# A two-block layer on one core: the last product by seven half products, a wide convolution, ScalarE's own gate function

## The chip, the cores and the metric

The kernel runs on one core of one Trainium2 chip. The core has engines that run side by side and wait for each other by semaphores: TensorE (PE) multiplies, VectorE (DVE) and ScalarE (ACT) do element-wise work, GpSimd (POOL) and SyncE (SP) here mostly issue DMAs; ACT issues DMAs too. Each engine takes its instructions strictly in the order in which they were built. The metric is the device time of one execution in microseconds, the median of several runs.

## What is computed

One input x of 1024 positions by 1024 channels goes through a hybrid layer (block 1: four branches, gates, an MLP) and then through block 2, which the change touches. Cut to what matters:

```python
def mix(h, lp, h0, pool_fn):
    proj = einsum('btd,de->bte', h, lp['w_in'])               # 1024 -> 11 slots of 512
    (va, za, bb, bc, bv, zb, ca, cg, zc, dv, zd) = split(proj, 11)
    ya, h_final = rglru(va, lp, h0)                            # mixer a
    yb = bb * depthwise_conv(bc * bv, lp['b_conv'])            # mixer b, 3 taps
    u = depthwise_conv(ca * sigmoid(cg), lp['c_conv'])         # mixer c, 31 taps
    u = layer_norm(u, ...)
    yc = einsum('btc,ce->bte', silu(u), lp['c_pw']) + lp['c_pw_b']
    yd = grouped_linear(pool_grid(dv)) * lp['d_scale']         # mixer d
    cat = concatenate([ya * silu(za), yb * silu(zb), yc * silu(zc), yd * silu(zd)])
    return einsum('bte,ed->btd', cat, lp['w_out'])             # 2048 -> 1024

x = x + gate * mix(h, ...)
return rms_norm(x, final_g)
```

## The kernel before, in words

Activations lie transposed, channels on the 128 partitions and positions along the row, so a tile of one channel group is 128 x 1024, and a half of it (512 positions, one PSUM bank) is called a half tile. Every fp32 product is made of three matmuls in fp32r: both operands are split into a high part (a cast on ACT) and the rest (a subtraction on DVE), and high by high, high by low and low by high are added up in PSUM (lines 411 to 413). One matmul has weights of 128 x 128 and 512 columns.

`mixers_in` (from line 2028) is block 2's input product: 44 weight blocks (11 slots by 4 channel groups), each with two halves of 24 matmuls, `mm<-kk,wh` in the rows. Between the groups `fill` advances generators: `self.bg` holds mixers a and d, and `convs` the 31-tap convolution of mixer c (`conv31`, line 2006 on). That convolution keeps two PSUM banks and adds one tap after the other into them on DVE, 512 columns at a time (line 2025), then copies the result back. Gates are made as 0.5 (1 + tanh(z/2)) z: a Tanh on ACT (lines 1991 and 2092) and a multiplication on DVE (lines 1992 and 2093). Each finished piece of `cat` (256 KB, `cz` or `sg` in the rows) is stored to DRAM by a DMA on ACT's queue.

`tail` (line 2216) is the last product. `dense(pair, hf)` runs four times, for two pairs of mixers and two halves of the positions: eight loads of `cat` (`cr<-cat`, SP's queue), their splits (`cx`, lines 469 and 470), then for each of eight output groups 24 matmuls and one DVE instruction that adds the result times the gate to x (line 2239). x itself was put into DRAM (`x2d`) and is loaded in the first two `dense` calls. `final` is the closing norm of one half.

Three small rings of tiles matter: half tiles (`F2`, six of them, shared by `pk`, `sg`, `cz` and `cr`), weights (three raw, three split) and PSUM (two `mm`, one `px`, five `pp` banks). A DMA into a tile of a ring waits until the tile's former content has been read, by a store too. `weight_sums` (line 1507) makes sums of weight blocks for the Strassen scheme that block 1's MLP uses already: on POOL's queue, load a block, add others by accumulating DMAs, store each partial sum to DRAM, all in one buffer `ws`.

The instructions of an engine do not stand in the order of the source: the framework reorders them when it builds the program, by its own estimates, so the order of the built program is shown below where it matters.

Of the kernel before, what the change touches and what calls it, by code (L numbers as in the profile page):

```python
# [17 lines left out]
P = 128  # L18
T = 1024
# [9 lines left out]
NL, N1, N2, N4, N3, FA, FB = 6.0, 3.0, 3.0, 2.4, 2.5, 4.0, 3.0  # L29
# [272 lines left out]
class Build:  # L302
    def __init__(self, tc, ctx, A, out, dbg=None):
# [16 lines left out]
        self.sums, self.paced = self.weight_sums(), 0  # L320
# [54 lines left out]
    def load_w(self, src, w=T):  # L375
# [3 lines left out]
        self.split(raw[:, :w], hi[:, :w], lo[:, :w])  # L379
        return hi, lo  # L380

    def weight_order(self):
# [9 lines left out]
        q += [("wo2", pair, n) for pair in range(2) for hf in range(2) for n in range(8)]  # L392
        self.wq, self.ahead = q, []

    def take(self, *key):
        if self.wq[0] is None:
            self.wq.pop(0)
        assert self.wq.pop(0) == key
        load = lambda name, *i: self.load_w(self.A[name][i] if name == "wup" else
                                               self.A[name][i].rearrange("p k n -> p (k n)"))  # L400
# [1106 lines left out]
    def weight_sums(self):  # L1507

        nc = self.nc
        A = self.A["wm2"]  # L1510
        self.ws = {n: [self.dp.tile([P, T], F32, name=f"{n}w{j}") for j in range(8)] for n in ("S1", "S2", "S3", "S4")}
        pin = self.tc.keep_in_program_order
        for j in range(8):
            block = lambda a, b: A[a, b][:, j * T:j * T + T]
            for first, *terms in (((1, 0), (1, 1), "S1", (0, 0), "S2", (0, 1), "S4"), ((0, 0), (1, 0), "S3")):
                t = self.wsp.tile([P, T], F32, tag="ws", name=self.nm("ws"))
                pin(nc.gpsimd.dma_start(t, block(*first)))
                yield
                for x in terms:
                    if isinstance(x, str):  # L1520
                        pin(nc.gpsimd.dma_start(self.ws[x][j], t))
                    else:
                        pin(nc.gpsimd.dma_start(t, block(*x), accum_op=ALU.add))
# [459 lines left out]
    def keep(self, slot, c, silu=False):  # L1983
# [15 lines left out]
    def cat_out(self, i, c, y, z, hf):  # L1999
# [3 lines left out]
        self.nc.vector.scalar_tensor_tensor(t, y, 0.5, t, op0=ALU.mult, op1=ALU.mult)  # L2003
        self.cat_store(i, c, t, hf)

# [5 lines left out]
    def conv31(self, c, u):  # L2011

        nc = self.nc
        w = lambda j: self.CW[:, 31 * c + j:31 * c + j + 1]
        acc = [self.pp(), self.pp()]
        for hf, sl in enumerate(HS):
            nc.vector.tensor_scalar(acc[hf], u[:, sl], w(15), None, op0=ALU.mult)
        for j in range(31):
# [3 lines left out]
            for hf in range(2):  # L2022
                a, b = max(HALF * hf, -s), min(HALF * hf + HALF, T - s)
# [292 lines left out]
```

## Time and profile before

| | |
|---|---|
| median of 3 runs | 2543.75 us (2543.48 to 2548.24) |
| profiled execution | 2544.9 us, of which the trace spans 2543.1 |
| PE busy | 2476.3 us, 97% of the span |
| DVE, ACT, POOL busy | 1727.1, 1188.1, 182.1 us (68%, 47%, 7%) |
| DMA traffic | 449 MB, 177 GB/s on average |
| mean granted clock of PE | 0.983 |

The trace of the profiled execution is read in four ways here: the page (totals), windows (busy time of each engine in a stretch, with the number of instructions, the granted clock and the DMA engines' share), timelines (single instructions with their start, their duration and, in brackets, how long the engine had been idle before and what released it), and lists of groups or transfers. Block 2's input product runs from about 1774 to 2329 us and the last product from 2333 to 2527; the closing norm takes the rest.

### The profile page before, as it was taken

The page shows a single profiled execution, that of the slowest core. Times are in us where ns is not written, and L with a number is a line of the kernel's source. Part 1 is how long each engine was busy: PE and PEld are TensorE (multiplying, and loading weights), DVE is VectorE, ACT ScalarE, POOL GpSimd, SP SyncE. Part 2 cuts the span into 40 slices and gives each one's busy share as a digit, 9 for nine tenths or more (in the row PEclk, how much of TensorE's full clock was granted, in tenths as well). Part 3 has the DMA queues.
Part 4 walks back from the last instruction along what each step waited for, and adds up shares of the span by engine and source line. Part 5 has one row for each costly group of instructions (what it writes and reads, how often), then busy time and mean ns, then how long its engine had stood idle before and what let it go on. Part 6 is the DMA issues. An engine that isn't in the chain of part 4 may idle for free. (4 is left out here: it accounts for less than half of the span.)

```text
span 2543.1 us, 33781 instructions
## 1 busy us (share of the span) xinstructions
PE 2476.3 (97%) x12732; PEld 2004.7 (79%) x12732; DVE 1727.1 (68%) x2647; ACT 1188.1 (47%) x1843; POOL 182.1 (7%) x238
## 2 busy tenths in 40 slices
PE   8999999999999999999999999999999999999997
PEld 7887888776777678877788888887888888887886
DVE  7536765664755436758867864457798999996744
ACT  5425554622514357147644543435536355445623
POOL 0000000120111111630000000000000000000000
PEclk9999999999999799999999999999999999999998
DMA  6365443683775567868676565556533333325732
GB/s 218 106 210 160 140 134 105 186 250 104 230 205 157 164 210 233 287 193 278 235 257 221 180 204 180 187 187 224 183 119 113 133 134 97 113 91 192 247 100 100
DMA packets 180085, 449.23 MB, mean 177 GB/s; under 512 B 32145, under 2 KB 42257, under 8 KB 179921
## 3 DMA queue, kind: packets, MB, share of 16 engines
q1 hardware_dynamic: 141504, 342.44, 40.5%
q0 software_dynamic: 18576, 64.63, 9.1%
q10 hardware_dynamic: 19840, 40.00, 4.3%
q8 instruction: 100, 1.64, 0.3%
q14 instruction: 65, 0.52, 0.1%
HBM read 321.55 MB, written 125.44 MB: 176 GB/s over the span
## 5 line engine op out<-in xcount | busy, mean ns | idle before, releaser
L367 ACT CAST wh<-wr 128x1024 fp32r<-128x1024 f32 x243 | 255.0, 1049 | 496.3 <-PE mm L412 246.5
L368 DVE TENSOR_TENSOR wl<-wr,wh 128x1024 fp32r<-128x1024 f32 x243 | 299.5, 1233 | 222.4 <-ACT wh L367 215.9
L411 PE MATMUL mm<-h,wh 128*128 128x512 f32 x760 | 308.1, 406 | 4.0 <-ACT h L469 2.1
L412 PE MATMUL mm<-h,wh 128*128 128x512 f32 x760 | 305.9, 403 | 0.8 <-DVE h L470 0.8
L413 PE MATMUL mm<-h,wl 128*128 128x512 f32 x760 | 304.7, 401 | 0.0
L411 PE MATMUL mm<-kk,wh 128*128 128x512 f32 x704 | 275.2, 391 | 0.0
L412 PE MATMUL mm<-kk,wh 128*128 128x512 f32 x704 | 274.5, 390 | 0.5 <-DVE kk L1811 0.5
L413 PE MATMUL mm<-kk,wl 128*128 128x512 f32 x704 | 274.0, 389 | 0.0
L411 PEld LDWEIGHTS mm<-h,wh 128*128 128x128 f32 x760 | 144.9, 191 | 37.2 <-ACT h L469 3.3
L412 PEld LDWEIGHTS mm<-h,wh 128*128 128x128 f32 x760 | 144.9, 191 | 33.7 <-issue 3.6
L413 PEld LDWEIGHTS mm<-h,wl 128*128 128x128 f32 x760 | 144.6, 190 | 32.7 <-issue 2.9
L2025 DVE SCALAR_TENSOR_TENSOR pp<-cu,vec,pp 128x512 f32<-128x512 f32 (+9 forms) x240 | 166.3, 746 | 0.1
L412 PEld LDWEIGHTS mm<-kk,wh 128*128 128x128 f32 x704 | 132.1, 188 | 29.1 <-issue 1.0
L411 PEld LDWEIGHTS mm<-kk,wh 128*128 128x128 f32 x704 | 132.1, 188 | 28.3 <-issue 0.7
L413 PEld LDWEIGHTS mm<-kk,wl 128*128 128x128 f32 x704 | 132.1, 188 | 27.7 <-issue 0.2
L1539 PE MATMUL pp<-h,wh 128*128 128x512 f32 x320 | 126.2, 397 | 3.8 <-ACT x L1606 2.2
L1540 PE MATMUL pp<-h,wh 128*128 128x512 f32 x320 | 124.8, 390 | 1.4 <-DVE h L470 1.4
L1541 PE MATMUL pp<-h,wl 128*128 128x512 f32 x320 | 123.6, 389 | 0.0
L1748 PE MATMUL pp<-bl,wh 128*128 128x512 f32 x304 | 120.1, 395 | 2.4 <-DVE bl L470 1.7
L1749 PE MATMUL pp<-bh,wl 128*128 128x512 f32 x304 | 119.1, 392 | 0.0
L1747 PE MATMUL pp<-bh,wh 128*128 128x512 f32 x304 | 116.5, 391 | 1.6 <-ACT bh L474 1.6
L411 PE MATMUL mm<-cx,wh 128*128 128x512 f32 x256 | 99.8, 391 | 1.3 <-ACT cx L469 1.3
(562 smaller groups left out, 5434.8 us busy)
## 6 DMA issues: line engine op xcount, KB each, us to landing
wr<-in_wi_dram SPq DMA_DIRECT2D x77, 512.0 KB, 3.4
ws<-in_wm_dram POOLq DMA_DIRECT2D x48, 512.0 KB, 5.8
wr<-in_wo_dram SPq DMA_DIRECT2D x48, 512.0 KB, 3.7
wr<-in_wg_dram SPq DMA_DIRECT2D x32, 512.0 KB, 4.4
gt<-gt POOLq DMA_DIRECT2D x64, 256.0 KB, 4.6
g<-gt SPq DMA_DIRECT2D x64, 256.0 KB, 4.9
wm<-in_wm_dram SPq DMA_DIRECT2D x32, 512.0 KB, 5.0
br<-buB SPq DMA_DIRECT2D x32, 512.0 KB
```

The costliest lines, as they stand in the source:

```text
L367: self.nc.scalar.copy(hi, raw)
L368: self.nc.vector.tensor_sub(lo, raw, hi.bitcast(F32))
L411: M(ps, lhsT=ah, rhs=bh, start=start and i == 0, stop=False)
L412: M(ps, lhsT=ah, rhs=bl, start=False, stop=False)
L413: M(ps, lhsT=al, rhs=bh, start=False, stop=stop and i == last)
L1539: M(ps, lhsT=ah, rhs=bh, start=start and i == 0, stop=False, skip_group_check=True)
L1540: M(ps, lhsT=ah, rhs=bl, start=False, stop=False, skip_group_check=True)
L1541: M(ps, lhsT=al, rhs=bh, start=False, stop=i == last, skip_group_check=True)
L1747: M(banks[p], lhsT=wh[:, o], rhs=bh[:, r], start=first, stop=False, skip_group_check=True)
L1748: M(banks[p], lhsT=wh[:, o], rhs=bl[:, r], start=False, stop=False, skip_group_check=True)
L1749: M(banks[p], lhsT=wl[:, o], rhs=bh[:, r], start=False, stop=jj == 7 and e == 1, skip_group_check=True)
L2025: nc.vector.scalar_tensor_tensor(o, u[:, a + s:b + s], w(j), o, op0=ALU.mult, op1=ALU.add)
```

## The change

1. The last product is done by Strassen's scheme over 2 x 2 blocks: the inputs are cut into two pairs of mixers (1024 channels each), the outputs into two groups of 512 channels, the positions into two halves. Seven products P1, P5, P2, P6, P7, P4, P3 of 4 output tiles x 8 operands x 3 matmuls take the place of eight. P1 stays in four PSUM banks and P2 is added onto it; P5 stays in four others until P3 is added; P6, P7 and P4 are added up in the first four again. Operands that are sums or differences of two pieces of `cat` are made by a load and an accumulating DMA on POOL's queue (`ct` and part of `cr`). The signs of the pieces are set where they are made (`sign_of`).
2. The weights of P5, P6, P7 and P3 are sums of blocks of `w_out`, made by a second `weight_sums` (4 output tiles): 40 more DMAs of 512 KB on POOL's queue.
3. x is loaded behind P1.
4. The convolution works in SBUF on 1023 columns or so at a time instead of 512 in PSUM, with its first tap on ACT; the LayerNorm and pointwise product of mixer c (`mixer_c`) are queued right behind the convolutions, not at the last loop's end.
5. The gates use ACT's Silu; the DVE multiplication of each goes.

```diff
-NL, N1, N2, N4, N3, FA, FB = 6.0, 3.0, 3.0, 2.4, 2.5, 4.0, 3.0
+NL, N1, N2, N4, N3, FA, FB = 6.0, 3.0, 3.0, 2.4, 2.5, 4.0, 4.0
...
             if silu:
-                nc.scalar.activation(t, ps, AF.Tanh, scale=0.5)
-                nc.vector.scalar_tensor_tensor(t, t, 1.0, ps, op0=ALU.add, op1=ALU.mult)
+                nc.scalar.activation(t, ps, AF.Silu)
...
-    def conv31(self, c, u):
+    def conv31(self, c, us):
...
-        acc = [self.pp(), self.pp()]
-        for hf, sl in enumerate(HS):
-            nc.vector.tensor_scalar(acc[hf], u[:, sl], w(15), None, op0=ALU.mult)
+        o = self.S("co")
+        nc.scalar.mul(o, u, w(15))
...
-            for hf in range(2):
-                a, b = max(HALF * hf, -s), min(HALF * hf + HALF, T - s)
-                o = acc[hf][:, a - HALF * hf:b - HALF * hf]
-                nc.vector.scalar_tensor_tensor(o, u[:, a + s:b + s], w(j), o, op0=ALU.mult, op1=ALU.add)
-            yield 1.3
-        for hf, sl in enumerate(HS):
-            nc.scalar.copy(u[:, sl], acc[hf])
+            a, b = max(0, -s), min(T, T - s)
+            nc.vector.scalar_tensor_tensor(o[:, a:b], u[:, a + s:b + s], w(j), o[:, a:b], op0=ALU.mult, op1=ALU.add)
+            yield 1.2
+        us[c] = o
...
+        self.sums = self.weight_sums(4, lambda a, b, j: self.A["wo2"][b, 4 * a + j].rearrange("p k n -> p (k n)"))
...
+            if c == 3:
+                convs.append(self.mixer_c(cus))
...
-            if c == 3:
-                while convs:
-                    self.tick(1, convs)
-                self.behind(self.mixer_c(cus))
...
     def tail(self):
...
-        def dense(pair, hf, ticks):
-            cx = HiLo.__new__(HiLo)
-            cx.t = [[], []]
-            for i in ((0, 3), (1, 2))[pair]:
-                for c in range(4):
-                    raw = self.F2("cr")
-                    nc.sync.dma_start(raw, self.cat[i, c, hf])
-                    t = self.S("cx", F32R)
-                    self.hilo(raw, t[:, 0:HALF], t[:, HALF:T])
-                    cx.t[hf].append(t)
...
+        run(self.sums)
+        ng = self.sm(8)
+        nc.vector.tensor_scalar(ng, self.MOD[:, 16:24, 0], -1.0, None, op0=ALU.mult)
+        cat = lambda b, c, k: self.cat[((0, 3), (1, 2))[b][k // 4], k % 4, c]
...
+        def source(p, k):
+            if p in ("P1", "P2", "P3", "P7"):
+                t = self.F2("cr")
+                nc.sync.dma_start(t, cat(*{"P1": (0, 0), "P2": (1, 0), "P3": (1, 1), "P7": (0, 1)}[p], k))
+                if p == "P7":
+                    nc.gpsimd.dma_start(t, cat(1, 1, k), accum_op=ALU.add)
+                return t
+            t = part(k)
+            if p == "P5" and k not in made:
+                nc.sync.dma_start(t, cat(0, 1, k))
+            elif p == "P5":
+                return t
+            made.add(k)
+            nc.gpsimd.dma_start(t, cat(*{"P5": (0, 0), "P6": (1, 1), "P4": (1, 0)}[p], k), accum_op=ALU.add)
+            return t
...
+        def add(a, c, j, ps, minus=False, done=False):
+
+            n = 4 * a + j
+            xa = x.get(n, c)
+            nc.vector.scalar_tensor_tensor(xa, ps, ng[:, n:n + 1] if minus else self.MOD[:, 16 + n, 0:1], xa,
+                                           op0=ALU.mult, op1=ALU.add)
...
+        run(ops["P1"])
+        for k in range(8):
+            source("P5", k)
+        A = bank_a()
+        for j, ps in product("P1", bs["P1"], A, True, ops["P5"], 6):
+            pass
         self.flush()
-        dense(1, 0, 0)
+        for hf in (1, 0):
+            self.load_x(x, hf, lambda hf, j: self.x2d[hf][j])
+        B = [self.pm.tile([P, HALF], F32, tag="mm", name=self.nm("mm")) for _ in range(2)]
+        B += [self.px.tile([P, HALF], F32, tag="px", name=self.nm("mm")), self.pp()]
+        for j, ps in product("P5", bs["P5"], B, True, ops["P2"]):
+            add(1, 1, j, ps)
+            add(1, 1, j, A[j])
+            add(1, 0, j, A[j])
+            add(0, 1, j, A[j], True)
+        for j, ps in product("P2", bs["P2"], A, False, ops["P6"]):
+            add(0, 0, j, ps, True, True)
+        A = bank_a()
+        for j, ps in product("P6", bs["P6"], A, True, ops["P7"]):
+            add(0, 1, j, ps)
...
```

In the built program, PE changes from the earlier work to the last product here before: `sc` are mixer c's operands, `cx` those of the last product, and `mm` and `pp` PSUM banks.

```order
L411 MATMUL pp_19979<-sc_19699,wch_19974 128x512
L412 MATMUL pp_19979<-sc_19699,wch_19974 128x512
L413 MATMUL pp_19979<-sc_19699,wcl_19975 128x512
L411 MATMUL mm_20117<-cx_20065,wh_19907 128x512
L411 MATMUL mm_20177<-cx_20065,wh_20113 128x512
L411 MATMUL mm_20233<-cx_20065,wh_20173 128x512
L412 MATMUL mm_20117<-cx_20065,wh_19907 128x512
L413 MATMUL mm_20117<-cx_20065,wl_19908 128x512
L412 MATMUL mm_20177<-cx_20065,wh_20113 128x512
L411 MATMUL mm_20117<-cx_20070,wh_19907 128x512
```

And here, on PE, in the change, where `kk` are the operands of the input product:

```order
L421 MATMUL mm_20085<-kk_16074,wh_19993 128x512
L422 MATMUL mm_20085<-kk_16074,wh_19993 128x512
L423 MATMUL mm_20085<-kk_16074,wl_19994 128x512
L2286 MATMUL pp_20177<-cx_20117,wh_20051 128x512
L2287 MATMUL pp_20177<-cx_20117,wh_20051 128x512
L2288 MATMUL pp_20177<-cx_20117,wl_20052 128x512
L2286 MATMUL pp_20177<-cx_20122,wh_20051 128x512
L2287 MATMUL pp_20177<-cx_20122,wh_20051 128x512
L2288 MATMUL pp_20177<-cx_20122,wl_20052 128x512
```

Before, three output groups share each operand and matmuls of mixer c follow among them; in the change all of mixer c stands ahead, the input product's last group is the last work before P1, and P1 takes its eight operands one after the other for one output group.

ACT, at the same place before (`sg` is the gate of mixer b, `cr` a loaded half tile of `cat`):

```order
L2092 ACTIVATE sg_19967<-mm_19942 128x512
L2144 ACTIVATE yc_19992<-pp_19979,vec 128x512
L469 CAST cx_20065<-cr_20063 128x512
L325 DMA cat_19971<-sg_19967 128x512
L469 CAST cx_20070<-cr_20068 128x512
L469 CAST cx_20075<-cr_20073 128x512
```

And ACT in the change:

```order
L367 CAST wh_20219<-wr_20217 128x1024
L325 DMA cat_19928<-cz_19925 128x512
L2101 ACTIVATE sg_20110<-mm_20085 128x512
L325 DMA cat_20113<-sg_20110 128x512
L479 CAST cx_20117<-cr_20118 128x512
L479 CAST cx_20122<-cr_20123 128x512
L479 CAST cx_20127<-cr_20128 128x512
```

The store of the last gate now stands ahead of all casts of P1's operands; before, the first cast stood ahead of it.

SP's queue in the change, from P1's fourth load on (`ct` holds two half tiles, which POOL's DMAs are added to; `S1w` are weight sums):

```order
L2245 DMA cr_20133<-cat_17205 128x512
L2245 DMA cr_20138<-cat_19575 128x512
L2245 DMA cr_20143<-cat_18850 128x512
L2245 DMA cr_20148<-cat_18211 128x512
L2245 DMA cr_20153<-cat_17550 128x512
L372 DMA wr_20345<-S1w_16042 128x1024
L2245 DMA cr_20380<-cat_18802 128x512
L2251 DMA ct_20157<-cat_19373 128x512
L2251 DMA ct_20157<-cat_18663 128x512
```

The load of `cr_20143` is P1's sixth, and the tile that it takes in the ring of six is that of `sg_20110`; the loads of P5's operands stand behind it on the same queue.

## Rows read from the trace of the kernel before

**Rows 1.** The page's totals: busy us (share of the span) and instructions of each engine.

```profile
PE 2476.3 (97%) x12732; PEld 2004.7 (79%) x12732; DVE 1727.1 (68%) x2647; ACT 1188.1 (47%) x1843; POOL 182.1 (7%) x238
```

**Rows 2.** Windows: stretch, busy PE, PEld, DVE, ACT, POOL (instructions), clock, DMA share, GB/s.

```profile
1015.00:1020.00 5.00, 2.74 (x8) 2.22 (x9) 5.00 (x12) 0.00 (x0) 0.00 (x0) 0.81 0.26 59
1280.00:1300.00 20.00, 20.00 (x90) 16.57 (x89) 13.20 (x18) 7.68 (x12) 0.00 (x0) 1.00 0.92 327
1940.00:1980.00 40.00, 40.00 (x178) 33.13 (x177) 39.92 (x50) 26.75 (x33) 2.55 (x3) 1.00 0.39 133
2420.00:2460.00 40.00, 40.00 (x178) 33.10 (x178) 15.04 (x16) 9.08 (x10) 0.00 (x0) 1.00 0.31 100
```

**Rows 3.** Timeline of PE: start, us, line, operation, tiles, [idle before and its releaser].

```profile
1017.26 0.50 PE L411 MATMUL mm<-br,wh 128*128 128x512 f32 x1 [3.10 <-DVE ma L1367]
...
2328.82 0.39 PE L413 MATMUL mm<-kk,wl 128*128 128x512 f32 x1
...
2333.27 0.97 PE L411 MATMUL mm<-cx,wh 128*128 128x512 f32 x3 [1.34 <-ACT cx L469]
...
2523.63 0.39 PE L413 MATMUL mm<-cx,wl 128*128 128x512 f32 x1
...
2527.03 0.39 PE L413 MATMUL mm<-cx,wl 128*128 128x512 f32 x1
```

**Rows 4.** Timeline of ACT where the last product begins.

```profile
2325.88 0.33 ACTq L325 DMA_DIRECT2D cat<-sg  x1
...
2329.01 1.05 ACT L367 CAST wh<-wr 128x1024 fp32r<-128x1024 f32 x1 [1.54 <-PE mm L412]
2329.97 0.59 ACT L2092 ACTIVATE sg<-mm 128x512 f32<-128x512 f32 x1
...
2335.54 2.37 ACT L469 CAST cx<-cr 128x512 fp32r<-128x512 f32 x4 [0.76 <-DVE cz L2003]
```

**Rows 5.** Timeline of DVE at the same place.

```profile
2330.10 1.23 DVE L368 TENSOR_TENSOR wl<-wr,wh 128x1024 fp32r<-128x1024 f32 x1 [1.91 <-ACT wh L367]
...
2331.96 0.69 DVE L2094 SCALAR_TENSOR_TENSOR sg<-by,sg 128x512 f32<-128x512 f32 x1
```

**Rows 6.** Timeline of SP's queue there, by two stretches; the second part of the first.

```profile
2328.63 6.73 SPq L2227 DMA_DIRECT2D cr<-cat  x5
...
2333.97 1.40 SPq L2227 DMA_DIRECT2D cr<-cat  x3
```

**Rows 7.** Loads of cr at 2315 to 2350: from issue to landing.

```profile
DMA to landing us min/median/max: 2.8/4.9/6.0
```

**Rows 8.** Transfers from 2000 on: count, KB each, median us from issue to landing.

```profile
cr<-cat SPq DMA_DIRECT2D x32, 256.0 KB, 5.3
...
cat<-cz ACTq DMA_DIRECT2D x22, 256.0 KB, 4.4
x<-x2d SPq DMA_DIRECT2D x8, 512.0 KB, 7.6
```

**Rows 9.** Timeline of POOL: two DMAs and a chain step; the sums' end; the next.

```profile
472.39 1.13 POOL L325 DMA_DIRECT2D gt<-gt  x2
479.74 0.94 POOL L1523 DMA_DIRECT2D ws<-in_wm_dram  x1 [6.22 <-DMA ws<-in_wm_dram]
...
1187.75 0.55 POOL L1521 DMA_DIRECT2D S3w<-ws  x1 [5.78 <-DMA ws<-in_wm_dram]
1856.92 0.53 POOL L325 DMA_DIRECT2D inv<-in_pinv_dram  x1 [668.62 <-DMA abr<-in_wab_dram]
```

**Rows 10.** Single lines: instructions, duration ns min/median/max, first and last start, forms.

```profile
L2025 DVE SCALAR_TENSOR_TENSOR pp<-cu,vec,pp x240: 729/747/765, 1847.4 to 2288.1; 128x512 f32<-128x512 f32 x68, 128x508 f32<-128x508 f32 x5, 128x497 f32<-128x497 f32 x4, 128x499 f32<-128x499 f32 x4
...
L1848 DVE SCALAR_TENSOR_TENSOR xc<-va,vec,xc x12: 1274/1282/1292, 1921.6 to 2195.5; 128x1023 f32<-128x1023 f32 x4, 128x1022 f32<-128x1022 f32 x4, 128x1021 f32<-128x1021 f32 x4
...
L1992 DVE SCALAR_TENSOR_TENSOR pk<-pk,mm x24: 656/682/697, 1934.6 to 2139.1; 128x512 f32<-128x512 f32 x24
```

**Rows 11.** Groups of ACT: table loads ahead of a gate, count, busy us, mean ns.

```profile
L1991 ACT ACT_TABLE_LOAD x3 | 3.8, 1283 | 0.5 <-ACT pk L1994 0.4
```

More of the change, by code (lines that the diff above doesn't have):

```diff
@@ L1499, in out_proj, with weight_sums @@
         self.behind(norm(1))
-    def weight_sums(self):
+    def weight_sums(self, count, block):
         nc = self.nc
-        A = self.A["wm2"]
-        self.ws = {n: [self.dp.tile([P, T], F32, name=f"{n}w{j}") for j in range(8)] for n in ("S1", "S2", "S3", "S4")}
+        ws = self.ws = {n: [self.dp.tile([P, T], F32, name=f"{n}w{count}{j}") for j in range(count)]
+                        for n in ("S1", "S2", "S3", "S4")}
         pin = self.tc.keep_in_program_order
-        for j in range(8):
-            block = lambda a, b: A[a, b][:, j * T:j * T + T]
+        for j in range(count):
             for first, *terms in (((1, 0), (1, 1), "S1", (0, 0), "S2", (0, 1), "S4"), ((0, 0), (1, 0), "S3")):
                 t = self.wsp.tile([P, T], F32, tag="ws", name=self.nm("ws"))
-                pin(nc.gpsimd.dma_start(t, block(*first)))
+                pin(nc.gpsimd.dma_start(t, block(*first, j)))
                 yield
@@ L2097, in mixers_in @@
             fill(FA, FB)
+        self.bg += convs
     def mixer_c(self, us):
@@ new lines, in tail, with part @@
+        ng = self.sm(8)
+        nc.vector.tensor_scalar(ng, self.MOD[:, 16:24, 0], -1.0, None, op0=ALU.mult)
+        cat = lambda b, c, k: self.cat[((0, 3), (1, 2))[b][k // 4], k % 4, c]
+        ct, made = [], set()
+        def part(k):
+            if k % 2 == 0 and len(ct) <= k // 2:
+                ct.append(self.S("ct"))
+            return ct[k // 2][:, HS[k % 2]]
+        def source(p, k):
[13 more added lines that the diff above has]
+            return t
@@ new lines, in operand @@
+        def operand(p, bs):
+            for k in range(8):
+                t = self.S("cx", F32R)
+                (self.hilo_minus if p in ("P7", "P4") else self.hilo)(source(p, k), t[:, 0:HALF], t[:, HALF:T])
+                bs.append(t)
+                if k % 2:
+                    yield
+        def add(a, c, j, ps, minus=False, done=False):
[3 more added lines that the diff above has]
+                                           op0=ALU.mult, op1=ALU.add)
+            if done:
+                first = accs[c] is None
+                if first:
+                    accs[c] = self.T2("acc")
+                self.add_sq(accs[c], xa, first)
@@ new lines, in product @@
+        def product(p, bs, banks, start, ahead=(), ticks=0):
+            M = nc.tensor.matmul
+            for j in range(4):
+                w = self.cols(self.take("o2", p, j))
+                ps = banks[j] if banks else self.mm()
+                for k in range(8):
+                    h, l = bs[k][:, 0:HALF], bs[k][:, HALF:T]
+                    M(ps, lhsT=w[0][k], rhs=h, start=start and k == 0, stop=False, skip_group_check=True)
+                    M(ps, lhsT=w[0][k], rhs=l, start=False, stop=False, skip_group_check=True)
+                    M(ps, lhsT=w[1][k], rhs=h, start=False, stop=k == 7, skip_group_check=True)
+                yield j, ps
+                next(iter(ahead), None)
```

62 lines of the change are left out of this document (34 added, 28 removed).

## The prediction

> **What bounds the kernel now.** I read the page first, then windows, then single rows. TensorE (PE) is busy for 2476 of 2543 us [rows 1], so time is won by taking matmuls away or by closing the few gaps. In the windows the reader should look at the last stage: at 2420 to 2460 PE is busy for the whole 40 us while VectorE (DVE) has 15 us of work, and at 1940 to 1980, in block 2's input product, PE is just as full although DVE is at 39.9 of 40 [rows 2]. So DVE is nearly saturated behind the input product, but PE does not wait for it. The rate of PE in the last product is read from two starts: fifteen matmuls later is 2527.03 - 2523.63 = 3.40 us later [rows 3], 0.2267 us for one. That is the unit of the sum.
>
> **Fewer matmuls.** The last product is now 2 x 2 x 8 x 8 x 3 = 768 matmuls, in the change 7 products x 4 x 8 x 3 = 672. 96 x 0.2267 = **21.8 us**, all of it on the engine that sets the end, in a stage where it is full.
>
> **How the first product begins.** This is the main loss. Before, the last product's first matmuls are interleaved with matmuls of mixer c (sc) and with three groups per operand, so operands that come late cost little: one wait of 1.34 us in front of 2333.27 [rows 3]. In the change nothing is left to interleave: the eight operands of P1 stand right behind the last group of the input product, and the ring of six half tiles hands the sixth load of P1 the tile of the last gate, so it waits until that gate's store has landed. I count from the start of the last matmul of the input product, T, which is 2328.82 before [rows 3]. ScalarE (ACT) then casts a weight (start T + 0.19, 1.05 us) and makes the gate (T + 1.15, 0.59 us) [rows 4]. DVE makes the weight's low part from T + 1.28 to T + 2.51 and then multiplies the gate, 0.69 us [rows 5]; of its two such instructions one goes, so the store issues at T + 3.2. A store of such a gate at 2325.88 [rows 4] let the next load start at 2328.63 [rows 6], 2.75 us later: the sixth load starts at T + 5.95. Loads of this kind take 2.8 us at least and 4.9 in the middle [rows 7]; here three that started from 2333.97 on [rows 6] fed casts that run from 2335.54 [rows 4], and nothing else is on SP's queue while it waits, so I take 2.8: T + 8.75, cast done (0.61) at T + 9.4. With no wait P1 would have begun at T + 0.23 and come to that operand 15 matmuls later, T + 3.63. The wait is 5.7, less the 1.34 that go: **4.4 us lost**. Upper bound, with the store at 4.4 and the load at the 6.0 of the slowest row [rows 7, 8]: T + 14.2, so 9.2 net. Lower bound, only the first cast behind the store (T + 3.8): 2.4. Behind that load on SP's queue stand the next two operands, a weight of P5 and P5's eight loads, all shifted with it.
>
> A wait of 3.7 us in front of P1 (T + 0.23 to about T + 3.9) is like the one before 1017.26, where PE had stood for 3.1 us [rows 3] and the granted clock of the next 5 us was 0.81, so at the lower of the two levels (1.2 GHz) for part of it [rows 2]. A stretch at half rate of about as long costs 1.7 us if matmuls are ready, but here the first five operands only run up to a sixth that isn't there. I take **0.5 us** (0 to 1.7).
>
> **P5's operands.** They come in two steps, a load on SP's queue and an accumulating one on GpSimd's (POOL). SP issues the eight loads from about T + 7.9 on; the last ones wait for earlier landings, to about T + 14.7. With 5.3 us for each load [rows 8] and 5.8 for each accumulating one (the store at 1187.75 waited that long for one of twice the size) [rows 9], the last lands at T + 26 to 28, cast and split by T + 29. One accumulation for P6 stands ahead of P5's last two on POOL's queue; it waits for the split of P5's first operand, T + 20.5, which is in these numbers. P1 ends at about T + 28 and P5 wants its last operand at T + 32.6: covered by 3 to 4 us. The loads of x (8 x 512 KB, 7.6 us each [rows 8]) move behind P1 and now run beside the accumulations. The third add of P5 waits on DVE for the seventh of them; queued behind it on DVE are splits of P2 and the low part of P5's last weight, wanted at T + 45. That add is reached at T + 35, and the load, issued about T + 21, should be there by T + 29 to 36. Covered by about 9 us. The cover is thin in the first case, so I take **1.0 us** (0 to 4).
>
> Here a page of the Trainium skill would give less: "DMA: Bandwidth & Descriptors", section "Anatomy of one DMA — SWDGE (gpsimd) path", fits a GpSimd DMA by 2.0 us plus its bytes at 436 GB/s, which by that page is an estimated 2.6 us for 256 KB; P5's operands would then stand 3 us earlier and its term would be 0. The trace speaks for longer times (5.8 us in rows 9 against 3.2 by the fit for 512 KB), so the sum goes by the rows.
>
> **Later products, sums of weights.** The operands of each later product are made during the one before, 21.8 us for eight pairs of DMAs: no cost if accumulations overlap (third rival). The 40 new POOL DMAs for the weight sums are a chain on one buffer; 28 stand right behind the last of the old sums, issued at 1187.75, and POOL does nothing after that until 1856.92 [rows 9]. At 5.8 us each they end near 1360. Their readers come after 2300. They move 14 MB beside a stage that reaches 327 GB/s with the DMA engines at 0.92 [rows 2]; PE is at 20.00 of 20 there, so weights have some lead. I take **0.5 us** (0 to 2). Three more stand in front of a memset of mixer d, whose reader is far behind.
>
> **Convolution, gates, adds.** 240 instructions of 0.747 us [rows 10] become 120 of about 1.27 (SBUF to SBUF over 1023 columns: 1.282) [rows 10] and 4 ACT scalings: 179 against 152 us, 27 saved, and six more by the dropped first taps. 32 gate instructions of 0.68 [rows 10] go, 22 us. Mixer c's remaining parts, some 28 us of DVE, move ahead of the tail. Net -27 us on an engine that PE does not wait for: **0 us**, bounds -3 to +2. The tail gains 24 splits (0.68) and 4 adds and loses mixer c; DVE stays below PE there. 11 more table loads at 1.28 us [rows 11] put 14 us on ACT, which is busy for 27 of 40 us at 1940 to 1980 [rows 2].
>
> **The sum.** 21.8 - 4.4 - 0.5 - 1.0 - 0.5 = 15.4 us. The profiled run before is 2544.9 us (span 2543.1 and 1.8 around it), so 2529.5; the median of the runs shown is 1.15 lower. Forecast: **2528.4 us**. All costs high: 21.8 - 9.2 - 1.7 - 4 - 2 - 2 = 2.9, 2540.9; all low: 21.8 - 2.4 + 3 = 22.4, 2521.4. I expect 2524 to 2536.
>
> **Rivals.**
> 1. *Full gain.* P1's sixth operand is not late (its loads start earlier because the scheduler's order leaves the gate's tile free sooner) and DVE's relief closes gaps in the input product: 21.8 to 24 us, 2519 to 2522. For it: PE's gaps there are small but exist. Against: the order of the built program shows the wait.
> 2. *The transfers bind.* From P1's sixth load to P5's last operand the queues carry about 7.1 MB, and x adds 4.2 beside it. At 327 GB/s [rows 2] that is 35 us instead of 22: P5's last operand at T + 42, 9 us late, and with the start near its upper bound 12 us are gone in all besides the terms above: 2536 to 2542. Against: x is issued last and need not win.
> 3. *Slower: accumulations run one at a time.* Then 32 of them are a chain from T + 11 on that must be through by P7's last operand, due at T + 98: it costs from 2.7 us each (87/32), and the change is slower than before from 3.4 each (87 + 15.4 + 5 over 32). At the 5.3 us of a 256 KB load [rows 8] it is 170 us, 83 late: 2611; at 4 us, 41 late: 2570. Against: two DMAs issued from 472.39 on were on POOL's queue beside a chain transfer that was waited for only 6.2 us, to 479.74 [rows 9]; but none of these accumulate beside one another, and no row shows that. The same page, section "SWDGE vs HWDGE vs iDMA", says that only one queue context of the software kind is allocated; if that meant one DMA at a time, this rival would hold. By the rows it does not.
> 4. *The gates' function costs more than it saves.* If the 14 us of table loads stood in front of PE: 2542. Against: PE did not wait for ACT's gates in the input product.
>
> **How the numbers follow.** Forecast 0.60, full gain 0.13, transfers 0.14, slower 0.09, table loads 0.04. A measurement of this kernel tells 0.2%, 5.1 us, from no change: faster is below 2538.7, slower above 2548.8. Faster: 0.60 + 0.13 + half of the second rival, 0.80; same 0.11; slower 0.09. The range leaves out the slow rival and a part of the outer cases: 2520 to 2541.
>
> **What would show it.** The tail with 96 fewer matmuls, 152 us of PE at 0.227 each; a gap of 3 to 4 us after the last input matmul and a second of 1 to 3 us before P1's sixth operand, both of which would be near zero if I am wrong on the ring; accumulating DMAs issued within a microsecond of each other and landing together; no PE gap between products; DVE some 27 us less busy from 1800 to 2330 with PE unchanged. I am wrong if PE waits in P5 to P7 for splits, or if the input product gets longer.

## The result and the profile after

The change is slower: median 2558.96 us (2547.23 to 2578.39, 11 runs) against 2543.48 us for the kernel before (2533.14 to 2551.95, 11 runs) in the same session, ratio 1.0057, 95% interval 1.0034 to 1.0081. The forecast was 2528.4 us, range 2520 to 2541. The profiled run of the change is 2560.85 us, its span 2559.1.

The page's totals of the changed kernel answer to [rows 1]: PE has 11.6 us less work and the span is 16 us longer.

```profile
PE 2464.7 (96%) x12636; PEld 1988.3 (78%) x12636; DVE 1698.5 (66%) x2512; ACT 1211.0 (47%) x1870; POOL 238.8 (9%) x310
```

A ledger by stages, from the starts of single matmuls in the two profiled runs, says where the time went. The input product's first matmul starts at 1811.7 us before and 1809.1 after; these 2.6 us were won earlier and mean nothing (the last section). From there to the last matmul of the last product it is 715.3 us before and 734.3 after, 19.0 more. The closing norm is the same (16.1 and 15.7).

- From the first matmul of the input product to the first of the last product: 521.6 us before with 24 of mixer c's 96 pointwise matmuls in it, 552.9 after with all 96. Less 0.2267 us for each of these, 516.1 and 531.1: **15.0 us lost**. Of these, 2.4 are the longer gap in front of P1 (4.17 us from start to start against 1.73), which the prediction had priced; the other 12.6 lie in the part that I had put at nothing.
- From the first to the last matmul of the last product: before 193.8 us for 840 matmuls, 190.4 of pure rate; after 181.4 us for 672, 152.3 of pure rate. The losses are 3.4 and 29.1: **25.7 us lost**, against the 21.8 us that the 96 matmuls give.

Windows of the change over its last product (stretch; busy PE, PEld, DVE, ACT, POOL with instructions; clock; DMA share; GB/s), against the full PE of [rows 2]. The reader should look at the second and the fourth: PE at 12.0 and 16.2 of 20 and the granted clock at 0.77 and 0.83; and in the first three at the DMA engines, at or over 1.0 with only 223 to 336 GB/s.

```profile
2380.00:2400.00 20.00, 18.50 (x72) 13.94 (x71) 8.94 (x11) 10.74 (x16) 8.89 (x10) 0.91 1.10 258
2400.00:2420.00 20.00, 11.98 (x45) 9.44 (x44) 10.66 (x16) 5.93 (x10) 0.00 (x0) 0.77 1.02 336
2420.00:2440.00 20.00, 19.47 (x83) 15.49 (x83) 15.25 (x22) 8.52 (x13) 9.35 (x11) 0.97 1.00 223
...
2460.00:2480.00 20.00, 16.16 (x60) 12.73 (x61) 18.00 (x26) 13.76 (x21) 0.00 (x0) 0.83 0.54 156
```

What PE waited for in the last product of the change (us in total, times, longest):

```profile
PE pp L2288 <- DVE wl L368: 8.5, 2, 8.0
PE pp L2286 <- ACT wh L367: 6.3, 1, 6.3
PE pp L2286 <- ACT cx L479: 3.8, 1, 3.8
```

The first is in P5. DVE's timeline shows it: the third add of P5 waits 7.7 us for a load of x, and the low part of P5's last weight (`wl` at 2414.48), which PE needs, is queued behind it. PE stood from 2407.3 to 2415.75; the granted clock of that window is 0.77.

```profile
2402.87 0.74 DVE L2271 SCALAR_TENSOR_TENSOR x<-pp,MOD,x 128x512 f32<-128x512 f32 x1
2411.35 0.75 DVE L2271 SCALAR_TENSOR_TENSOR x<-pp,MOD,x 128x512 f32<-128x512 f32 x1 [7.74 <-DMA x<-x2d]
...
2412.68 1.88 DVE L480 TENSOR_TENSOR cx<-cr,cx 128x512 fp32r<-128x512 f32 x3
2414.48 1.22 DVE L368 TENSOR_TENSOR wl<-wr,wh 128x1024 fp32r<-128x1024 f32 x1
```

The second is in P6. On ACT the casts of P7's operands wait 11.75 us for accumulated tiles, and the cast of a weight that P6 needs (`wh` at 2462.32) stands behind them. The last two of these accumulations were issued only at 2452.26 and 2454.24, when the plain loads into the same tiles had landed, and took 6.9 us each.

```profile
2459.26 0.63 ACT L484 ACTIVATE cx<-cr 128x512 fp32r<-128x512 f32 x1 [11.75 <-DMA cr<-cat]
2461.26 0.63 ACT L484 ACTIVATE cx<-cr 128x512 fp32r<-128x512 f32 x1 [1.37 <-DMA cr<-cat]
...
2462.32 1.03 ACT L367 CAST wh<-wr 128x1024 fp32r<-128x1024 f32 x1
```

Why x and the tiles were late is in the list of transfers from 2372 to 2412: each queue's bytes with the time that its packets took as a share of 16 engines, then count, size and median landing. The accumulating DMAs (q0) moved 4.20 MB and took 57.6% of the engines for 40 us, 23.0 us; the plain ones (q1) moved 7.53 MB in 50.5%, 20.2 us. That is 182 against 373 GB/s: an accumulated byte holds the DMA engines about twice as long. (The shares add up to more than 100%, so some packets overlap.) The loads of x land after 17.4 us instead of 7.6 [rows 8] (the trace gives the landing of two of the eight, 15.3 and 19.6 us), the accumulations after 11.6.

```profile
q0 software_dynamic: 2304, 4.20, 57.6%
q1 hardware_dynamic: 2685, 7.53, 50.5%
...
ct<-cat POOLq DMA_DIRECT2D x16, 256.0 KB, 11.6
x<-x2d SPq DMA_DIRECT2D x8, 512.0 KB, 17.4
```

The loads of x were also issued late, and that too goes back to the accumulations. On ACT the cast of a weight (`wh` at 2384.63) stands behind casts of `ct` that had waited for them, 8.75 us for the first. On SP's queue the next load of a weight waited 12.4 us for that weight's split, and x stands behind it: its first load went out at 2387.38, 25.4 us after P1's first matmul.

```profile
2380.08 0.62 ACT L479 CAST cx<-ct 128x512 fp32r<-128x512 f32 x1 [8.75 <-DMA ct<-cat]
...
2384.63 1.05 ACT L367 CAST wh<-wr 128x1024 fp32r<-128x1024 f32 x1
```

```profile
2386.96 0.32 SPq L372 DMA_DIRECT2D wr<-S1w  x1
2387.38 6.67 SPq L1431 DMA_DIRECT2D x<-x2d  x8
```

PE's waits in the input product and up to the first matmul of P1 are these; before, there were 1.5 us (two waits for `ph`) and 0.5, and the 1.34 of [rows 3]. With one more of 0.5 for `kk` they add up to 12.8 us, against 3.3.

```profile
PE mm L421 <- ACT bm L2087: 4.5, 1, 4.5
PE pp L2286 <- ACT cx L479: 3.8, 1, 3.8
PE pp L421 <- ACT ph L479: 1.9, 2, 1.4
PE pp L422 <- DVE pl L480: 1.2, 1, 1.2
PE mm L423 <- DVE wl L368: 0.9, 1, 0.9
```

The largest: `bm` is ACT's copy of mixer b's slot out of PSUM. On ACT it stands behind mixer c's norm (`lt`, `ln`, `sc`) and its table loads, which in turn go back and forth with DVE. PE stood from 2253.6 to 2258.5 and the six us after that were granted 0.50, which cost about 3 us more. So 9.5 and 3 of the 15.0 us are found; the remaining 2.5 are not put down to single rows.

```profile
2250.66 1.28 ACT L2138 ACT_TABLE_LOAD   x1
2251.95 1.34 ACT L2138 ACTIVATE lt<-ln,sm 128x512 f32<-128x512 f32 x2
2253.20 1.32 ACT L2139 ACTIVATE ln<-ln,vec 128x512 f32<-128x512 f32 x2
2254.96 0.72 ACT L2138 ACTIVATE lt<-ln,sm 128x512 f32<-128x512 f32 x1 [0.45 <-DVE ln L2136]
...
2257.86 0.56 ACT L2087 COPY bm<-mm 128x512 f32<-128x512 f32 x1
```

### The profile page after: what moved, and what is told of

It is laid out like the page before. It is cut to its first block, busy times and chain, and to the rows that moved or that the text cites. A ratio compares the mean times of both kernels' runs of the same rounds, so it can differ in the third digit from the quotient of the medians.

```text
span 2559.1 us, 33598 instructions
## 1 busy us (share of the span) xinstructions
PE 2464.7 (96%) x12636; PEld 1988.3 (78%) x12636; DVE 1698.5 (66%) x2512; ACT 1211.0 (47%) x1870; POOL 238.8 (9%) x310
## 3 DMA queue, kind: packets, MB, share of 16 engines
q1 hardware_dynamic: 142080, 342.44, 40.4%
## 4 chain that ended last, share of the span: by engine, by line
PE 66%; DVE 14%; DMA 9%; ACT 6%; issue 3%; SPq 1%; POOL 1%; ACTq 0%; DVEq 0%; POOLq 0%
PE mm L422 8%; PE mm L421 8%; PE mm L423 8%; PE pp L1548 3%; PE pp L1550 3%; PE pp L1549 3%; DVE co L2036 3%; PE pp L421 2%; PE pp L422 2%; PE pp L423 2%; PE pp L1757 2%; PE pp L1758 2%; PE pp L1756 2%; DMA cr<-cat 2%; PE pp L644 2%
## 5 line engine op out<-in xcount | busy, mean ns | idle before, releaser
L367 ACT CAST wh<-wr 128x1024 fp32r<-128x1024 f32 x235 | 246.2, 1049 | 427.6 <-PE mm L422 155.7
L368 DVE TENSOR_TENSOR wl<-wr,wh 128x1024 fp32r<-128x1024 f32 x235 | 289.1, 1232 | 215.6 <-ACT wh L367 212.1
L422 PEld LDWEIGHTS mm<-kk,wh 128*128 128x128 f32 x704 | 132.4, 188 | 29.6 <-issue 1.4
L2036 DVE SCALAR_TENSOR_TENSOR co<-cu,vec,co 128x1009 f32<-128x1009 f32 (+14 forms) x120 | 152.8, 1273 | 3.2 <-ACT co L2030 2.1
L1300 ACT ACTIVATE gt<-mm,bgh 128x512 f32<-128x512 f32 x64 | 43.6, 685 | 102.6 <-PE mm L423 97.8
```

What stands on the lines that cost most here:

```text
L367: self.nc.scalar.copy(hi, raw)
L368: self.nc.vector.tensor_sub(lo, raw, hi.bitcast(F32))
L422: M(ps, lhsT=ah, rhs=bl, start=False, stop=False)
L2036: nc.vector.scalar_tensor_tensor(o[:, a:b], u[:, a + s:b + s], w(j), o[:, a:b], op0=ALU.mult, op1=ALU.add)
```

## The experiments

Eleven kernels ran, all beside the kernel before. Times are medians of 10 or 11 runs; the ratio is to the kernel before on the same chip. In a table first, with the stage ledger from each profiled run (A: first matmul of the input product to the last of the last product; B: the last product alone):

| run | median us | ratio, 95% interval | A us | B us |
|---|---|---|---|---|
| before | 2543.5 to 2545.1 | | 715.3 | 193.8 |
| the change | 2558.96 | 1.0057 (1.0034 to 1.0081) | 734.3 | 181.4 |
| e1 last product only | 2561.64 | 1.0063 (1.0029 to 1.0098) | 729.1 | 182.7 |
| e2 mixers only | 2561.31 | 1.0057 (1.0028 to 1.0087) | 730.5 | 177.7 |
| e3 no accumulation | 2541.95 | 0.9991 (0.9962 to 1.0020) | 710.4 | 155.8 |
| e4 addition on DVE | 2543.81 | 1.0002 (0.9974 to 1.0030) | 713.6 | 161.2 |
| e5 wide convolution only | 2549.19 | 1.0030 (0.9994 to 1.0065) | 719.5 | 194.1 |
| e6 Silu only | 2549.80 | 1.0018 (0.9988 to 1.0049) | 720.4 | 197.6 |
| e7 mixer c's place only | 2557.01 | 1.0055 (1.0023 to 1.0087) | 725.6 | 208.0 |
| e8 wide, place and `FB`, Tanh | 2559.81 | 1.0065 (1.0030 to 1.0099) | 734.5 | 179.2 |
| e9 gate in the other ring | 2548.66 | 1.0028 (1.0003 to 1.0052) | 716.5 | 153.0 |
| e10 e4 and e9 together | 2530.43 | 0.9952 (0.9933 to 0.9970) | 703.3 | 153.0 |
| e11 and taps counted 1.0 | 2527.30 | 0.9929 (0.9904 to 0.9955) | 701.7 | 153.0 |

B is only comparable among e3, e4, e9 to e11 and the change (672 matmuls, none of mixer c's); in before, e5 and e6 it holds 768 and 72 of mixer c's, in e7 768 and 96, in e2 and e8 768, in e1 672 and 48.

One more edit belongs to the mixers' half and is not in the list of the change, only in its diff: `FB`, the credit that `fill` gives the queue of the convolutions behind each group, goes from 3.0 to 4.0. The change, e2 to e4 and e8 to e11 have 4.0; before, e1, e5, e6 and e7 have 3.0. Counted from the code, the four convolutions are then through after 25 of the 36 calls of `fill` that use it, instead of 34. No run has this edit alone.

**The two halves apart.** e1 keeps the last product of the change and undoes the mixers, `FB` and the convolution included:

```diff
-            nc.scalar.activation(t, ps, AF.Silu)
+            nc.scalar.activation(t, ps, AF.Tanh, scale=0.5)
+            nc.vector.scalar_tensor_tensor(t, t, 1.0, ps, op0=ALU.add, op1=ALU.mult)
...
-            if c == 3:
-                convs.append(self.mixer_c(cus))
+            if c == 3:
+                while convs:
+                    self.tick(1, convs)
+                self.behind(self.mixer_c(cus))
```

> The change without its other half: Strassen tail, weight sums and signs as in the change, but the convolution in PSUM on 512 columns, Tanh gates and mixer c's place as before. The changed kernel's input product lost about 12.6 us (PE, from its first gap at 1815 us to the first matmul of P1) and its tail 25.7 us against 152 us of matmuls. Theory M (the convolution, the gates or mixer c's new place lose the 12.6): the input product is as before, the tail is as bad, total 2545 to 2549 us; a few less if mixer c's matmuls in the tail fill its waits. Theory S (the weight sums on GpSimd's queue in the middle of the input product lose them): as the change, 2557 to 2561.

e2 is the reverse, the mixers of the change in the kernel before:

```diff
-                nc.scalar.activation(t, ps, AF.Tanh, scale=0.5)
-                nc.vector.scalar_tensor_tensor(t, t, 1.0, ps, op0=ALU.add, op1=ALU.mult)
+                nc.scalar.activation(t, ps, AF.Silu)
...
+        o = self.S("co")
+        nc.scalar.mul(o, u, w(15))
...
+            if c == 3:
+                convs.append(self.mixer_c(cus))
```

> The other half alone: wide convolution, Silu gates, mixer c queued behind the convolutions; last product by eight full products as before, no weight sums of w_out. Theory M: slower than before by about 12 us, 2554 to 2558, with the 4.9 us wait for ACT's copy in front of mixer b and a stretch at half clock behind it. Theory S: within 2 us of before, 2541 to 2546.

e2 measured +16 us and shows the change's waits in the input product to a tenth:

```profile
PE mm L411 <- ACT bm L2072: 4.5, 1, 4.5
PE mm L411 <- ACT cx L469: 3.8, 1, 3.8
```

There are no sums of `w_out` in it, so theory S falls: the weight sums don't cause these waits. The stretch from 1180 us to the input product, beside which 28 of the sums run, took 630.9 us before, 631.9 in the change and 631.1 in e2, so they cost about 1 us (the stretch begins with the first matmul after 1180 us whose operand is `h`). e1 missed what theory M expected (2545 to 2549): it is as slow as the change. With mixer c at its old place its norm and products are not done when the input product ends. In the kernel before, the last product's groups run among them; here half of mixer c's 96 matmuls stand ahead of P1 and the others inside it. PE waits for mixer c in the gap:

```profile
PE pp L421 <- ACT wch L367: 8.0, 2, 5.1
PE mm L2292 <- ACT wh L367: 6.4, 1, 6.4
PE pp L2129 <- DVE la L2127: 6.3, 1, 6.3
```

So the move of mixer c and the seven products are not independent: without the move the new last product has to wait for mixer c, with it the input product does.

**Which transfers.** e3 leaves the accumulating DMAs of the last product out, so that operands that should be sums are single pieces:

```diff
-                if p == "P7":
-                    nc.gpsimd.dma_start(t, cat(1, 1, k), accum_op=ALU.add)
...
-            nc.gpsimd.dma_start(t, cat(*{"P5": (0, 0), "P6": (1, 1), "P4": (1, 0)}[p], k), accum_op=ALU.add)
```

> The change with its 32 accumulating DMAs of the last product left out (the operands are then not sums). Theory T (the transfers bind: accumulating DMAs fill the DMA engines, x's loads land 16 to 24 us after their issue, VectorE waits for them with a weight of P5 behind): waits of 8.0 and 6.3 us in P5 and at P7 go, with their half-clock stretches, 14 to 18 us faster than the change: 2541 to 2545. Theory X (x is late because it is loaded late, whatever runs beside it): only the second wait goes, 2551 to 2554.

It measured 2541.95: 17 us faster than the change, and the last product takes 155.8 us, with no long wait of PE left but the one at P1's beginning. The loads of x, which stand in the same place of the program, were issued 12.1 us after P1's first matmul instead of 25.4 and land after 10.5 us. So x was loaded late and landed late, and both came from the accumulations; theory X, by which it is late whatever runs beside it, falls. But the result didn't say whether the bytes or the accumulating counted. e4 brings in the same bytes by plain loads and adds on DVE:

```diff
+        def plus(t, src):
+            u = self.F2("cs")
+            nc.sync.dma_start(u, src)
+            nc.vector.tensor_add(t, t, u)
...
-                    nc.gpsimd.dma_start(t, cat(1, 1, k), accum_op=ALU.add)
+                    plus(t, cat(1, 1, k))
```

> The change with each accumulating DMA replaced by a plain load on SyncE's queue and an addition of 128x512 on VectorE (0.69 us each, 22 us over the tail). The number of bytes brought in is the same. Theory T in the form that an accumulation takes the DMA engines twice as long as a plain load: x lands earlier, 6 to 14 us faster than the change, 2545 to 2553. If only the number of bytes counted: same as the change, 2557 to 2561, or slower by VectorE's additions.

It measured 2543.81, 15 us faster than the change and a little better than expected. The same stretch of its trace: 13.57 MB in 90.2% of the engines, 36.1 us, so 376 GB/s, and x is issued 14.6 us after P1's first matmul and lands after 9.5 us. The 22 us of additions that DVE got cost one wait of 3.0 us in P5, for a weight's low part.

```profile
q1 hardware_dynamic: 5449, 13.57, 90.2%
...
x<-x2d SPq DMA_DIRECT2D x8, 512.0 KB, 9.5
```

e4 also moves these transfers from POOL's queue to SP's, so the queue could be the reason instead of the accumulating. The trace of before speaks against it. From 471 to 479.7 us POOL's queue carried three plain stores (`gt`) and one plain load and no accumulation: 1.29 MB in 36.2% of 8.7 us, 410 GB/s, beside 380 on q1.

```profile
q1 hardware_dynamic: 417, 1.51, 45.7%
q0 software_dynamic: 371, 1.29, 36.2%
```

**Which of the mixers' edits.** e5 has the wide convolution alone, e6 Silu alone, e7 mixer c's new place alone, all three with `FB` at 3.0; e8 has the wide convolution, the place and `FB` at 4.0. The diffs are pieces of the change, on the kernel before:

```diff
-            for hf in range(2):
-                a, b = max(HALF * hf, -s), min(HALF * hf + HALF, T - s)
+            a, b = max(0, -s), min(T, T - s)
```

> The kernel before with the wide convolution alone (SBUF to SBUF, first tap on ACT); gates by Tanh, mixer c's norm and product queued where they were. The mixers' half lost 15 us in the input product, in traces 4.5 us in one wait for ACT's copy of mixer b, about 3 us of half clock behind it, 2.4 at the start of the last product and some 3.4 in four waits for mixers a and d. Theory P (mixer c's new place does it: its norm stands on ACT ahead of that copy): no loss, within 3 us of before, 2541 to 2547. Theory D (the wide instructions, 1.27 us each, make other engines wait longer for VectorE): the four small waits are here, 3 to 5 us, 2547 to 2551.

```diff
-                nc.scalar.activation(t, ps, AF.Tanh, scale=0.5)
+                nc.scalar.activation(t, ps, AF.Silu)
```

> The kernel before with ScalarE's Silu alone for the gates. Theory P: within 3 us of before, 2542 to 2548. Theory L (the added table loads stand in front of copies that free PSUM): the 4.5 us wait for ACT is here, 2549 to 2556.

```diff
-                self.behind(self.mixer_c(cus))
...
+                convs.append(self.mixer_c(cus))
...
+        self.bg += convs
```

> The kernel before with mixer c's norm and product queued right behind the convolutions (what is left goes behind the input product), nothing else changed. Theory P: the 4.5 us wait for ACT, its half-clock stretch and the later start of the last product are here, 10 to 15 us slower than before, 2554 to 2560. Theories D and L: within 3 us of before, 2542 to 2548.

The first and the third diff and `FB` at 4.0 together are e8.

> The mixers' half without its gates: wide convolution and mixer c's new place, Tanh as before. Theory P: as the mixers' half, 2556 to 2562. Theory L (Silu's table loads do it): within 4 us of before, 2542 to 2549.

e5 and e6 came out 4 and 5 us above before; their intervals include no change. e8 gives the whole loss (+15) without Silu, so theory L falls as the cause. e7 alone is clearly slower too (+12 us), by the number that theory P expected, but it doesn't test theory P, because its edit did not bring mixer c forward. At three taps behind each group the convolutions are through only near the end, and what is left of mixer c goes behind the input product. Counted from the start of the last matmul of the input product, the norm's first Tanh (`lt`) begins 18.5 us ahead before, 5.7 ahead in e7 and 104.6 ahead in e8 (105.8 in the change), and mixer c's first matmul 10.3 ahead before, 11.3 behind in e7 and 94.6 ahead in e8. The rows are those of before, e7 and e8; the first start is the figure to look at, and the last matmul of the input product starts at 2328.8, 2338.1 and 2370.1.

```profile
L2129 ACT ACTIVATE lt<-ln,sm x8: 707/716/728, 2310.3 to 2368.3; 128x512 f32<-128x512 f32 x8
L2128 ACT ACTIVATE lt<-ln,sm x8: 708/720/727, 2332.4 to 2401.5; 128x512 f32<-128x512 f32 x8
L2125 ACT ACTIVATE lt<-ln,sm x8: 705/722/726, 2265.5 to 2336.0; 128x512 f32<-128x512 f32 x8
```

So e7 lost its time with a later mixer c, not an earlier one. The wait for ACT's copy is not there at all; PE waits at the beginning of the last product instead, for the first operands and a weight of mixer c:

```profile
PE mm L411 <- ACT cx L469: 3.8, 2, 3.5
PE pp L411 <- ACT wch L367: 2.3, 1, 2.3
```

In e8, where mixer c does come early, the copy's wait is back (4.0 us) and there are 6.0 us for low parts of weights on DVE:

```profile
PE mm L413 <- DVE wl L368: 6.0, 3, 2.9
PE mm L411 <- ACT bm L2073: 4.0, 1, 4.0
```

So the mixers' loss comes with an early mixer c in every run that has one. How much of it the place and `FB` alone would give, without the wide convolution, was not run.

**The beginning of P1.** e9 is the change with the gate tile that P1's sixth load waited for taken from a ring with eight tiles:

```diff
-                t = self.F2("sg")
+                t = self.T2("sg") if c == 3 else self.F2("sg")
```

> The change with the last gates of mixer b in another ring of tiles (eight T2 tiles), so that P1's sixth load no longer waits for the last gate's store. My theory of the first product's beginning: the 4.2 us gap ahead of P1, the half clock behind it and the wait at the sixth operand go (the change took 4.2 + 24.7 us there, of which 21.8 are matmuls), 5 to 7 us faster than the change, 2552 to 2554. If the sixth load is not what P1 waits for, at most the gap shrinks a little: 2557 to 2560.

It measured 10 us less than the change. P1 follows the input product without a gap, and the last product takes 153.0 us although all 32 accumulations are kept: the loads of x now begin 20 us ahead of P1 (2372.0 and 2391.7) and no longer 25 behind its start (2387.4 and 2362.0). But the accumulations still bind, in another place. They now run beside the end of the input product, P5's casts wait on ACT for them, and behind these casts stands the cast of a weight of mixer c (2383.49). PE waited 11.3 us for it in one piece:

```profile
2377.84 0.62 ACT L479 CAST cx<-ct 128x512 fp32r<-128x512 f32 x1 [1.42 <-DMA ct<-cat]
2382.96 0.62 ACT L479 CAST cx<-ct 128x512 fp32r<-128x512 f32 x1 [4.51 <-DMA ct<-cat]
...
2383.49 0.61 ACT L367 CAST wch<-wcr 128x512 fp32r<-128x512 f32 x1
```

e10 takes both: e4's plain loads and e9's ring.

> Both: accumulations replaced by loads and additions on VectorE, and the last gates in the other ring. If the two are independent, E4's 2543.8 less 5 to 9 us: 2535 to 2539. If P5 then waits for its operands instead (they are shifted with P1): 2541 to 2544.

2530.43: 13 us below e4 and 18 below e9, and faster than the kernel before (0.9952, interval 0.9933 to 0.9970). The two ends of its last product are 2503.63 - 2350.65 = 152.98 us apart for 671 steps, 0.228 each, and PE goes from the input product into P1 without a break:

```profile
2350.42 0.39 PE L423 MATMUL mm<-kk,wl 128*128 128x512 f32 x1
2350.65 0.39 PE L2291 MATMUL pp<-cx,wh 128*128 128x512 f32 x1
...
2503.63 0.39 PE L2293 MATMUL pp<-cx,wl 128*128 128x512 f32 x1
```

e11 changes one number more, the credit that a tap of the convolution costs in `fill`, and with it the order of the input product, by one group: six taps instead of five stand behind each of the first four:

```diff
-            yield 1.2
+            yield 1.0
```

> The same with the convolution's taps counted 1.0 instead of 1.2 in the filling of the input product, so that more of them stand behind each group and mixer c's norm comes earlier. If the 15 us that the mixers' half lost hang on where its pieces fall among the groups (ACT's copy for mixer b behind mixer c's norm), another order changes them: 5 to 12 us less than the kernel with 1.2, 2524 to 2533. If they hang on the amount of work, nothing: 2535 to 2539.

2527.30, the fastest of all (0.9929, interval 0.9904 to 0.9955), but its gain over e10, 3 us, is less than expected and within the spread of the runs. The wait for ACT's copy is gone and others stand in its place (3.8 us for a weight of mixer c, 2.2 for mixer d), so the stage is only 1.6 us shorter. So an order without that one wait was found, and most of the mixers' loss stayed. What bounds the input product then is not settled: several short waits on ACT and DVE add up, and no run took them away together.

## Why the prediction was wrong, step by step

- **The unit and the count** were right: 96 fewer matmuls at 0.2267 us. e9 to e11 run the 672 in 153.0 us.
- **The beginning of P1** was right in mechanism and nearly in size. Forecast: a wait of 3.7 us in front of P1, then half clock under the wait for the sixth operand, 4.9 us net in all. Measured: a wait of 3.79 us (4.17 from start to start, 1.73 before), a granted clock of 0.69 from 2364 to 2368, and P1 took 24.7 us instead of 21.8, where the last product before lost 1.1 in its first 96 matmuls: 4.2 us net. e9's ring took the gap and P1's 2.9 us away. What I missed is what else that ring holds up: the loads of all later operands and of x shift with it, and e9's last product has no wait.
- **P5's operands and x** is the step that failed, the term that was mis-sized most: 1.0 us (0 to 4) against 14.9 (counted by 96 matmuls, P5 took 36.7 us). I named the very wait, DVE's third add with P5's last weight behind it, and called it covered by 9 us, because I let x's loads begin at T + 21 (T is the start of the input product's last matmul) and priced them at the 7.6 us of [rows 8], a stretch without accumulations. They began at T + 29.6, held up on SP's queue behind a weight's load that waited for a split, whose cast stood behind casts of accumulated tiles; and they took 15 to 20 us. P5's own operands came late too (the last cast at T + 35.0, where I had it split by T + 29), but PE waited only 1.5 us for them. The third add came at T + 53.6, where I had x there by T + 36 and the weight behind it wanted at T + 45. The trace of before had the number that was needed: its transfer list (share of 16 engines beside bytes) gives the software queue 9.1% for 64.63 MB and the hardware queue 40.5% for 342.44 MB, 279 against 332 GB/s, when only a quarter of q0's bytes (32 steps of 512 KB of the old sums, 16.8 MB) were accumulating. I looked at landing times and issues only. The second rival had the mechanism in part ("the transfers bind", at 327 GB/s and 9 us), at a chance of 0.14; it priced all bytes alike.
- **Later products at no cost** was wrong: P6 took 31.3 us, 9.5 more than its matmuls, by the wait for accumulated tiles on ACT. The third rival asked whether accumulations overlap. They are under way together but land one after the other: six were issued within 5.4 us from 2372.33 on, landings came 7.5 to 16.5 us after issue, in the order of issue and 1.1 to 2.6 us apart, 2.6 while x was loading. The rival priced one at a time at 4 to 5.3 us each and said that it costs from 2.7 on; its form was wrong, its worry was right in a milder form: they share the engines, and each byte counts double. The one queue context of which the Trainium skill speaks ("DMA: Bandwidth & Descriptors", "SWDGE vs HWDGE vs iDMA") did not keep six from being under way at once here. The Trainium skill's fit on the same page ("Anatomy of one DMA — SWDGE (gpsimd) path") would give an estimated 2.6 us for each; the median was 11.6 here, with 16 of them beside 7.5 MB of other traffic.
- **Mixers at 0 us** was wrong by 12.6 (15.0 less the 2.4 of the gap in front of P1). The step said that DVE gets 27 us less work and PE does not wait for it. DVE's work did fall (its busy time by 29 us on the page), but I counted amounts and not places. The new place of mixer c and `FB` at 4.0, which the prediction doesn't price, put its norm, with table loads and handovers between ACT and DVE, among instructions that free PSUM or make weights, and PE waits for these in order. The built order that I had in hand shows `bm` behind `lt`, `ln`, `sc` on ACT; I looked there at P1's place and at POOL only. The rows show 4.5 us of this and the half clock behind it; that the rest comes the same way is argued, not shown.
- **Weight sums** at 0.5 us were right (about 1 us), and for Silu with its table loads e6 measured 5 us, with an interval that includes none.

The sum of the ledger: -21.8 + 15.0 + 25.7, and 0.1 of rounding, is the 19.0 us by which the two stages grew. Both things that the prediction named as signs of being wrong were there: PE waited in P5 and P6, and the input product got longer.

## What to carry to other kernels

Price a DMA by the engine time per byte of its kind, not by its landing time in a quiet stretch: an accumulating DMA took twice as long per byte, and 32 plain loads with additions on a VectorE that had room made this kernel 15 us faster. When work moves between stages, look on every in-order engine at what stands behind it: three of the four large waits were a weight's cast or split or a PSUM copy queued behind other work of its engine, in two of them work that waited for a transfer. And a ring of tiles that holds one load also holds every load behind it on the queue; moving the last gates to another ring was worth 10 to 13 us. When an experiment moves a piece of work, read in its trace where the piece went before reading its time: e7's went the other way.

## What the runs showed of the hardware that was not expected

- An accumulating DMA into SBUF held the DMA engines for 23.0 us per 4.20 MB (182 GB/s), a plain load in the same stretch for 20.2 us per 7.53 MB (373 GB/s). Plain transfers on the same software queue ran at 410 GB/s in the kernel before, so it is the accumulating that costs.
- The sixteen accumulating DMAs issued from 2372 to 2395 were under way together and landed in the order of issue, 1.1 to 2.6 us apart, 7.5 to 16.5 us after their issue.
- The time of one and the same kernel spreads much more than the three runs before the prediction showed (2543.48 to 2548.24): 31 runs of the kernel before lay between 2530.1 and 2557.3 us in one session, 31 between 2530.0 and 2565.3 in another. The time goes with the mean granted clock: 2530.92 us at 0.989 and 2550.94 at 0.981 in one session. In the profiled runs block 1 is where they differ: the input product of block 2 begins at 1800.3 us in e10 and at 1828.2 in e9, whose code is the same up to the last product. Up to there both ran the same matmuls, at a mean granted clock of 0.99 and 0.97. So 0.2%, which I took as the limit of a measurement, needs more than ten runs of each here. The stretch of e10, then that of e9 (the third figure from the right is the clock):

```profile
0.00:1800.30 1800.30, 1752.64 (x9620) 1415.21 (x9621) 1130.16 (x1880) 851.88 (x1397) 186.07 (x246) 0.99 0.63 203
```

```profile
0.00:1828.20 1828.20, 1777.95 (x9621) 1432.56 (x9622) 1129.93 (x1880) 852.20 (x1397) 186.71 (x246) 0.97 0.62 200
```
